# Seven products for eight: Strassen's scheme in three of eight K pairs of five 1024-column blocks

## The chip, the cores and the metric

The kernel runs on one core of one Trainium2 chip. The metric is the device time of one execution in microseconds (us). Engines are named as in the profile: PE is TensorE (PEld its weight loads), DVE VectorE, ACT ScalarE, SP the engine whose queue issues most DMAs.

## The reference

One decoder sub-layer on x of 256 tokens by 2048 channels, in float32:

```python
h = rms_norm(x, g_pre) * (1.0 + scale) + shift
proj = einsum('bsd,de->bse', h, w_in)            # 20032 columns
q_mla, kv_a, z_mla, qkv_dil, z_dil, gl_mla, gl_dil = split(proj, IN_SPLITS)
a  = mla_branch(q_mla, kv_a, ...) * silu(z_mla)
y_mla = einsum('bse,ed->bsd', a, w_mla_proj)
bb = dilated_branch(qkv_dil, ...) * silu(z_dil)
y_dil = einsum('bse,ed->bsd', bb, w_dil_proj)
merged = sigmoid(gl_mla) * y_mla + sigmoid(gl_dil) * y_dil
out = einsum('bsd,de->bse', merged, w_o)
x = x + gate * rms_norm(out, g_post)
```

The change touches three of the matrix products, each with K = 2048: the gate logits `gl_mla` (h by 2048 columns of w_in), the latent output `y_mla` (a by w_mla_proj), and the first 1024 of the 2048 columns of `out` (merged by w_o).

## The kernel before, in words

Every product of 256 tokens by a weight matrix is computed at float32 accuracy from float32r parts. Both operands are split into a high part (rounded to float32r) and a low part (the rest), and three matmul phases are summed: high by high, low activation by high weight, high activation by low weight. The token side (`hT`, `aT`, `mT`: the transposed activations, 16 K tiles of 128 rows by 256 tokens, in tiles `...h` and `...l`) is split once. The weight side is streamed: `load_split` (L243 to L253) loads two K tiles by 512 columns (512 KB) into a `raw` buffer (8 of them), ACT casts it to `whi` (L251), DVE subtracts to get `wlo` (L252); there are 4 buffers each of `whi` and `wlo`. `multiply` (L255) then issues 12 matmuls of 128x512: 3 phases, 2 K tiles, 2 token halves.

```python
for ph in range(3):
    wt = wlo if ph == 2 else whi
    part = opd.lo if ph == 1 else opd.hi
    for k in range(nk):
        for t in ts:
            T.matmul(acc[:, t, :n], opd.get(part, k0 + k, t), wt[:, k * n:(k + 1) * n], ...
```

`group` (L283) does this for 8 such chunks into one accumulator of two PSUM banks (`acc`, two accumulators in all), so one 512-column group is 96 matmuls. Four further banks (`b`) serve transposes and attention.

The end of the program runs, in this order: four pairs of groups `gd` and `yd`, which give `part`; four groups `gm` of gate logits (L797 to L801; ACT takes the sigmoid out of PSUM); four groups `ym` (L803 to L813), where DVE multiplies the accumulator with the sigmoid (L805), adds it to `part` (L806), PE transposes the sum (`pt_m`, L448) and it is split into `mTh` and `mTl` (L438, L439); `gate_finish` (L350 to L362) makes the output gate `gg` from two DMAs `bg`, issued on ACT's queue, and two PE products `pt_g`. Then four groups `o0` to `o3` of the output projection (L838 to L843) and a last one, followed by the norm and the store.

A scheduler in the tile framework puts each engine's instructions in order and adds the semaphore waits; each engine executes its own list in that order.

Of the kernel before, what the change touches and what calls it, by code (L numbers as in the profile page):

```python
# [73 lines left out]
def hybrid_block(ctx: ExitStack, tc: tile.TileContext, x, c, positions, w_ada, b_ada, g_pre, g_post,  # L74
                 w_in, g_kv, w_kv_b, w_mla_proj, w_dil_proj, w_o, table, out):
    nc = tc.nc
    V, A, T = nc.vector, nc.scalar, nc.tensor
# [719 lines left out]
    for n in range(4):  # L797
        acc = group(hT, win, KC, C_GLM + n * 512, 512, f"gm{n}")
        sg = slot([P, 2, 512], f"sgm{n}")
        A.activation(sg, acc, AF.Sigmoid)  # L800
        sgm.append(sg)  # L801
    mT_h, mT_l = [], []
    for n in range(4):  # L803
# [3 lines left out]
        hi = slot([P, 4, S], f"mTh{n}", F32R)  # L807
        lo = slot([P, 4, S], f"mTl{n}", F32R)
        transpose_split(part[n], hi, lo, f"m{n}")
        mT_h.append(hi)  # L810
        mT_l.append(lo)
        if n < 2:
            gate_finish(n)  # L813
# [72 lines left out]
```

## Time and profile before

| what | value |
|---|---|
| time, median of 3 runs | 1281.7 us (1280.17 to 1281.78) |
| the profiled execution: its own time | 1281.44 us |
| its span (first to last instruction) | 1279.7 us |
| PE busy | 1260.7 us, 99% of the span, 6101 instructions |
| PEld busy | 1050.0 us, 82% |
| DVE busy | 814.8 us, 64%, 1201 instructions |
| ACT busy | 601.9 us, 47%, 778 instructions |
| chain that ended last | PE 98%, DVE 1% |
| granted TensorE clock, mean | 0.995 |
| HBM | 214 GB/s over the span |

The span is what the profiler saw between the first and the last instruction; the execution's own time is 1.7 us longer. Busy time is the time in which an engine executed at least one instruction; instructions of DVE and ACT overlap their neighbours a little, so the sum of the single durations is larger than the busy time. The chain that ended last is followed back from the last instruction: at each step to the instruction whose end released it, or to the one before it on its engine.

### The profile page before, as it was taken

The page shows a single profiled execution, that of the slowest core. Times are in us where ns is not written, and L with a number is a line of the kernel's source. Part 1 is how long each engine was busy: PE and PEld are TensorE (multiplying, and loading weights), DVE is VectorE, ACT ScalarE, POOL GpSimd, SP SyncE. Part 2 cuts the span into 40 slices and gives each one's busy share as a digit, 9 for nine tenths or more (in the row PEclk, how much of TensorE's full clock was granted, in tenths as well). Part 3 has the DMA queues.
Part 4 walks back from the last instruction along what each step waited for, and adds up shares of the span by engine and source line. Part 5 has one row for each costly group of instructions (what it writes and reads, how often), then busy time and mean ns, then how long its engine had stood idle before and what let it go on. Part 6 is the DMA issues. An engine that isn't in the chain of part 4 may idle for free.

```text
span 1279.7 us, 16445 instructions
## 1 busy us (share of the span) xinstructions
PE 1260.7 (99%) x6101; PEld 1050.0 (82%) x6101; DVE 814.8 (64%) x1201; ACT 601.9 (47%) x778; POOL 0.2 (0%) x4
## 2 busy tenths in 40 slices
PE   7999999999999999999999999999999999999997
PEld 3788888888888888888888888888888888888886
DVE  4878887897984645556566576664544444565545
ACT  3556334433374544464554555555544444434442
POOL 0000000000000000000000000000000000000000
PEclk9999999999999999999999999999999999999999
DMA  9999988987554566656577585775566666666741
GB/s 329 313 304 334 317 277 281 309 269 233 171 160 119 156 190 195 185 158 215 164 223 243 171 281 175 225 229 161 154 196 196 192 191 196 206 214 187 256 155 67
DMA packets 158172, 275.01 MB, mean 215 GB/s; under 512 B 9542, under 2 KB 46860, under 8 KB 158092
## 3 DMA queue, kind: packets, MB, share of 16 engines
q1 hardware_dynamic: 156276, 268.43, 67.9%
q10 hardware_dynamic: 1816, 5.53, 1.2%
q8 instruction: 48, 0.79, 0.2%
q14 instruction: 32, 0.26, 0.1%
HBM read 271.83 MB, written 2.10 MB: 214 GB/s over the span
## 4 chain that ended last, share of the span: by engine, by line
PE 98%; DVE 1%; DMA 0%; ACT 0%; issue 0%; DVEq 0%; SPq 0%; ACTq 0%
PE acc_d L262 31%; PE acc_mq L262 10%; PE acc_zm L262 7%; PE acc_gd L262 7%; PE acc_ym L262 7%; PE acc_gm L262 7%; PE acc_o L262 6%; PE acc_kv L262 3%; PE acc_yd L262 3%; PE acc_zd L262 3%; PE acc_kva L262 2%; PE pv_D L543 1%; PE s_D L525 1%; PE s_M L722 1%; PE row L186 1%; PE pt_pD L487 1%
## 5 line engine op out<-in xcount | busy, mean ns | idle before, releaser
L251 ACT CAST whi_d<-raw_d 128x1024 fp32r<-128x1024 f32 (+1 forms) x156 | 152.7, 986 | 182.5 <-PE acc_d L262 138.7
L252 DVE TENSOR_TENSOR wlo_d<-raw_d,whi_d 128x1024 fp32r<-128x1024 f32 (+1 forms) x156 | 176.4, 1139 | 72.6 <-ACT whi_d L251 70.9
L262 PE MATMUL acc_d<-whi_d,hTh 128*128 128x512 f32 x576 | 160.2, 396 | 1.4 <-DVE d L636 1.4
L262 PE MATMUL acc_d<-whi_d,hTl 128*128 128x512 f32 x576 | 157.2, 391 | 0.0
L262 PE MATMUL acc_d<-wlo_d,hTh 128*128 128x512 f32 x576 | 156.2, 390 | 0.0
L262 PEld LDWEIGHTS acc_d<-whi_d,hTl 128*128 128x128 f32 x576 | 108.5, 189 | 23.8 <-DVE hTl L229 0.8
L262 PEld LDWEIGHTS acc_d<-wlo_d,hTh 128*128 128x128 f32 x576 | 108.4, 188 | 22.9
L262 PEld LDWEIGHTS acc_d<-whi_d,hTh 128*128 128x128 f32 x576 | 106.3, 188 | 22.7 <-issue 1.8
L252 DVE TENSOR_TENSOR wlo_mq<-raw_mq,whi_mq 128x1024 fp32r<-128x1024 f32 x48 | 58.7, 1223 | 49.4 <-ACT whi_mq L251 44.6
L193 DVE SCALAR_TENSOR_TENSOR ada<-raw_a,ccol,ada 128x512 f32<-128x512 f32 (+1 forms) x96 | 77.4, 807 | 17.1 <-DMA raw_a<-in_w_ada 16.0
L251 ACT CAST whi_mq<-raw_mq 128x1024 fp32r<-128x1024 f32 x48 | 50.4, 1050 | 59.6 <-PE acc_mq L262 26.9
L252 DVE TENSOR_TENSOR wlo_gm<-raw_gm,whi_gm 128x1024 fp32r<-128x1024 f32 x32 | 39.2, 1225 | 45.4 <-ACT whi_gm L251 45.4
L252 DVE TENSOR_TENSOR wlo_gd<-raw_gd,whi_gd 128x1024 fp32r<-128x1024 f32 x32 | 39.2, 1224 | 37.3 <-ACT whi_gd L251 37.3
L252 DVE TENSOR_TENSOR wlo_zm<-raw_zm,whi_zm 128x1024 fp32r<-128x1024 f32 x32 | 39.2, 1224 | 33.5 <-ACT whi_zm L251 27.5
L252 DVE TENSOR_TENSOR wlo_ym<-raw_ym,whi_ym 128x1024 fp32r<-128x1024 f32 x32 | 39.1, 1222 | 32.1 <-ACT whi_ym L251 32.1
L251 ACT CAST whi_ym<-raw_ym 128x1024 fp32r<-128x1024 f32 x32 | 33.7, 1055 | 51.0 <-PE acc_ym L262 41.0
L251 ACT CAST whi_gm<-raw_gm 128x1024 fp32r<-128x1024 f32 x32 | 33.8, 1055 | 49.6 <-PE acc_gm L262 43.9
L252 DVE TENSOR_TENSOR wlo_o<-raw_o,whi_o 128x1024 fp32r<-128x1024 f32 x28 | 34.2, 1224 | 35.4 <-ACT whi_o L251 32.4
L262 PE MATMUL acc_mq<-whi_mq,hTh 128*128 128x512 f32 x192 | 55.2, 409 | 0.0
L251 ACT CAST whi_gd<-raw_gd 128x1024 fp32r<-128x1024 f32 x32 | 33.6, 1051 | 40.9 <-PE acc_gd L262 18.7
L251 ACT CAST whi_zm<-raw_zm 128x1024 fp32r<-128x1024 f32 x32 | 33.6, 1051 | 39.5 <-PE acc_zm L262 12.5
L262 PE MATMUL acc_mq<-whi_mq,hTl 128*128 128x512 f32 x192 | 51.6, 391 | 0.0
(279 smaller groups left out, 2352.2 us busy)
## 6 DMA issues: line engine op xcount, KB each, us to landing
raw_d<-in_w_in SPq DMA_DIRECT2D x132, 512.0 KB, 4.5
raw_mq<-in_w_in SPq DMA_DIRECT2D x48, 512.0 KB, 4.5
raw_a<-in_w_ada SPq DMA_DIRECT2D x80, 256.0 KB, 4.7
raw_zm<-in_w_in SPq DMA_DIRECT2D x32, 512.0 KB, 4.2
raw_g<-in_w_ada SPq DMA_DIRECT2D x32, 512.0 KB, 4.4
raw_gd<-in_w_in SPq DMA_DIRECT2D x32, 512.0 KB, 4.4
raw_gm<-in_w_in SPq DMA_DIRECT2D x32, 512.0 KB, 4.4
raw_ym<-in_w_mla_proj SPq DMA_DIRECT2D x32, 512.0 KB, 3.9
```

Source lines behind the costliest of these rows:

```text
L186: T.matmul(row[0:1, j, 0:n], ccol[:, kk:kk + 1], v[:, k, j, :], start=kk == ROW_K[0], stop=kk == ROW_K[-1])
L193: V.scalar_tensor_tensor(flat, w, ccol[:, kk:kk + 1], flat, op0=ALU.mult, op1=ALU.add)
L251: A.copy(whi[:, :m], raw[:, :m])
L252: V.tensor_tensor(wlo[:, :m], raw[:, :m], whi[:, :m].bitcast(F32), ALU.subtract)
L262: T.matmul(acc[:, t, :n], opd.get(part, k0 + k, t), wt[:, k * n:(k + 1) * n], start=start and ph == 0 and k == 0, stop=stop and ph == 2 an ...
L487: T.transpose(pt[:, b, :], sm[:, (b0 + b) * P:(b0 + b + 1) * P], ident)
L525: T.matmul(sc[:, i * nk:(i + 1) * nk], qk[g][:, 0, t * P:(t + 1) * P], qk[g][:, 1, 0:nk], start=True, stop=True)
L543: T.matmul(pv, pT[:, b, :], dil[2, g, quad][:, kt, hs], start=b == 0, stop=b == nb - 1)
L722: T.matmul(sc[:, o:o + nk], qk[:, 0, t * P:(t + 1) * P], qk[:, 1, 0:nk], start=True, stop=False)
```

## The change

For five blocks of 1024 columns (two of `gm`, two of `ym`, the first half of the output projection) the two 512-column groups are computed together by `two_groups`. K goes in eight pairs of K tiles, and the string `PLAN = "SNSNSNNN"` says how each is done. An N pair is as before: two chunks (one for each 512 columns), 24 matmuls. An S pair is Strassen's scheme (Winograd's form) on the 2x2 blocks of the pair: K tile by token half on the one side, K tile by 512 columns on the other. It has seven products of three matmuls each, 21 in all. Its weight side needs four sums of raw weights (L359, L360, L363, L364, in place in the `raw` buffers) and four splits: `c` (512 columns), `d`, `e` and `f` (1024 each), which take one `whi` and one `wlo` buffer each. Four of the products gather in banks of their own (`p_...0` to `p_...3`, all four `b` banks), three in the accumulators. The token side needs sums too (`sums_of`): for each of the three S pairs a full-precision tile `af`, four sums `as`, and their split `ap`; they are made for h, a and merged once each, nine times in all. At the end of a block the banks are combined: one copy on ACT (L375), four additions of 512 columns and two of 1024 on DVE (L376 to L381). The sigmoid (L908), the product (L914) and the sum (L915) then follow as before, from SBUF. `gate_finish` is called once a block. The pool of small tiles `sp` is closed before `gm` and reopened as `sp2`.

```diff
+PLAN = "SNSNSNNN"
...
+    def products(bank, a, b, start, stop):
+
+        for i, (x, y) in enumerate(((a[0], b[0]), (a[1], b[0]), (a[0], b[1]))):
+            T.matmul(bank, x, y, start=start and i == 0, stop=stop and i == 2)
+
+    def sums_of(opd, i, name):
+
+
+        q, b = divmod(2 * i, 4)
+        full = slot([P, 2, S], f"af_{name}{i}")
+        V.tensor_add(full, opd.hi[q][:, b:b + 2, :].bitcast(F32), opd.lo[q][:, b:b + 2, :].bitcast(F32))
+        tmp = slot([P, 4, P], f"as_{name}{i}")
+        a11, a12, a21, a22 = [full[:, k, t * P:(t + 1) * P] for k in range(2) for t in range(2)]
+        V.tensor_add(tmp[:, 0, :], a12, a22)
+        V.tensor_sub(tmp[:, 1, :], tmp[:, 0, :], a11)
+        V.tensor_sub(tmp[:, 2, :], a11, a12)
+        V.tensor_sub(tmp[:, 3, :], a21, tmp[:, 1, :])
+        parts = sp.tile([P, 2, 4, P], F32R, tag="ap", bufs=5, name=f"ap_{name}{i}")
+        split(parts[:, 0], parts[:, 1], tmp)
+        return parts
...
+            first, final = i == first_s, i == last_s
+            (b11,) = both(r1, 512, "c")
+            products(banks[0], a(0, 0), b11, first, final)
+            V.tensor_sub(r1[:, l], r1[:, h], r1[:, l])
+            V.tensor_sub(r1[:, h], r2[:, h], r1[:, h])
+            b21, b22 = both(r2, 1024, "d")
+            t1, t3 = both(r1, 1024, "e")
+            V.tensor_sub(r2[:, h], r2[:, h], r1[:, l])
+            V.tensor_sub(r2[:, l], r2[:, l], r2[:, h])
+            products(banks[1], sm(0), t1, first, final)
+            products(banks[3], sm(2), t3, first, final)
+            t4, t2 = both(r2, 1024, "f")
+            products(banks[2], sm(1), t2, first, final)
+            products(acc[0][:, 1, :], a(1, 1), t4, begin((1, 0)), False)
+            products(acc[0][:, 0, :], a(1, 0), b21, begin((0, 0)), False)
+            products(acc[1][:, 0, :], sm(3), b22, begin((0, 1)), False)
+            tick()
+
+        u = [slot([P, 2, 512], f"u_{name}{j}") for j in range(2)]
+        A.copy(u[0][:, 0, :], banks[0])
+        V.tensor_add(u[1][:, 1, :], u[0][:, 0, :], banks[2])
+        V.tensor_add(u[0][:, 1, :], u[1][:, 1, :], banks[3])
+        V.tensor_add(u[1][:, 0, :], u[1][:, 1, :], banks[1])
+        V.tensor_add(u[1][:, 1, :], u[0][:, 1, :], banks[1])
+        for j in range(2):
+            V.tensor_add(u[j], u[j], acc[j])
+        return u
...
-    for n in range(4):
-        acc = group(aT, w_mla_proj[0], KC, n * 512, 512, f"ym{n}")
-        V.tensor_mul(sgm[n], sgm[n], acc)
-        V.tensor_add(part[n], part[n], sgm[n])
...
+    for m in range(2):
+        for j, y in enumerate(two_groups(aT, sums_a, w_mla_proj[0], KC, m * 1024, f"ym{m}")):
+            n = 2 * m + j
+            V.tensor_mul(sgm[n], sgm[n], y)
+            V.tensor_add(part[n], part[n], sgm[n])
...
+        gate_finish(m)
     mT = Opd(mT_h, mT_l)
...
+    sums = sums_for(mT, "m")
+    made = two_groups(mT, sums, w_o[0], KC, 0, "o")
     for i, (c0, n) in enumerate(blocks[:-1]):
-        acc = acc_tile(f"acc_o{i}")
-        run(acc, mT, w_o[0], 0, KC, c0, n, f"o{i}")
+        if i < 2:
+            acc = made[i]
+        else:
+            acc = acc_tile(f"acc_o{i}")
+            run(acc, mT, w_o[0], 0, KC, c0, n, f"o{i}")
```

What this does to the order is shown at the opening of the output projection. First DVE's list there before the change, from the last `wlo` of group `ym3` on (`o0_0`, `o0_2` ... are chunks of the output projection, `acc_ym3` the last accumulator of the stage before):

```order
L252 TENSOR_TENSOR wlo_ym3_14_9673<-raw_ym3_14_9670,whi_ym3_14_9672 128x1024
L252 TENSOR_TENSOR wlo_o0_0_9723<-raw_o0_0_9720,whi_o0_0_9722 128x1024
L252 TENSOR_TENSOR wlo_o0_2_9741<-raw_o0_2_9738,whi_o0_2_9740 128x1024
L252 TENSOR_TENSOR wlo_o0_4_9759<-raw_o0_4_9756,whi_o0_4_9758 128x1024
L805 TENSOR_TENSOR sgm3_9028<-sgm3_9028,acc_ym3_9543 128x1024
L252 TENSOR_TENSOR wlo_o0_6_9777<-raw_o0_6_9774,whi_o0_6_9776 128x1024
L806 TENSOR_TENSOR sgd3_8366<-sgd3_8366,sgm3_9028 128x1024
L252 TENSOR_TENSOR wlo_o0_8_9795<-raw_o0_8_9792,whi_o0_8_9794 128x1024
L439 TENSOR_TENSOR mTl3_9691<-pt_m30_9692,mTh3_9690 128x512
L439 TENSOR_TENSOR mTl3_9691<-pt_m31_9699,mTh3_9690 128x512
L252 TENSOR_TENSOR wlo_o0_10_9813<-raw_o0_10_9810,whi_o0_10_9812 128x1024
```

And DVE's list at the same place in the changed kernel, from the sum of the first half of the second `ym` block (`u_ym10`) on; `e` and `f` are splits of the first S pair of the output projection:

```order
L381 TENSOR_TENSOR u_ym10_9869<-u_ym10_9869,acc_ym10_9548 128x1024
L347 TENSOR_TENSOR wlo_oe0_9993<-raw_oa0_9975,whi_oe0_9992 128x1024
L914 TENSOR_TENSOR u_gm20_9159<-u_gm20_9159,u_ym10_9869 128x1024
L381 TENSOR_TENSOR u_ym11_9870<-u_ym11_9870,acc_ym11_9549 128x1024
L915 TENSOR_TENSOR sgd2_8145<-sgd2_8145,u_gm20_9159 128x1024
L914 TENSOR_TENSOR u_gm21_9160<-u_gm21_9160,u_ym11_9870 128x1024
L347 TENSOR_TENSOR wlo_of0_10005<-raw_ob0_9977,whi_of0_10004 128x1024
L543 TENSOR_TENSOR mTl2_9881<-pt_m20_9882,mTh2_9880 128x512
L543 TENSOR_TENSOR mTl2_9881<-pt_m21_9889,mTh2_9880 128x512
L915 TENSOR_TENSOR sgd3_8366<-sgd3_8366,u_gm21_9160 128x1024
L543 TENSOR_TENSOR mTl3_9899<-pt_m30_9900,mTh3_9898 128x512
L543 TENSOR_TENSOR mTl3_9899<-pt_m31_9907,mTh3_9898 128x512
```

Before, whole chunks of the output projection were split between the steps of the combination; now two splits of its first S pair (`e`, `f`) stand among ten steps of the combination. Three rows on (one chunk's split and the gate's additions), DVE's list reaches the token-side sums:

```order
L466 TENSOR_TENSOR gg1_9914<-gg1_9914,bg11_9923 128x1024
L295 TENSOR_TENSOR af_m0_9939<-mTh0_9502,mTl0_9503 128x512
L298 TENSOR_TENSOR as_m0_9941<-af_m0_9939 128x128
L300 TENSOR_TENSOR as_m0_9941<-af_m0_9939 128x128
L299 TENSOR_TENSOR as_m0_9941<-as_m0_9941,af_m0_9939 128x128
L295 TENSOR_TENSOR af_m2_9949<-mTh1_9520,mTl1_9521 128x512
L301 TENSOR_TENSOR as_m0_9941<-af_m0_9939,as_m0_9941 128x128
L298 TENSOR_TENSOR as_m2_9951<-af_m2_9949 128x128
L300 TENSOR_TENSOR as_m2_9951<-af_m2_9949 128x128
L299 TENSOR_TENSOR as_m2_9951<-as_m2_9951,af_m2_9949 128x128
L295 TENSOR_TENSOR af_m4_9959<-mTh2_9880,mTl2_9881 128x512
L543 TENSOR_TENSOR ap_m0_9946<-as_m0_9941,ap_m0_9946 128x512
```

All rows but the first are new; `ap_m0`, the split of the sums for the first S pair, is the last of them. On PE the output projection began before the change with

```order
L262 MATMUL acc_o0_9719<-whi_o0_0_9722,mTh0_9177 128x512 x4
L262 MATMUL acc_o0_9719<-whi_o0_0_9722,mTl0_9178 128x512 x4
L262 MATMUL acc_o0_9719<-wlo_o0_0_9723,mTh0_9177 128x512 x4
L262 MATMUL acc_o0_9719<-whi_o0_2_9740,mTh0_9177 128x512 x4
L262 MATMUL acc_o0_9719<-whi_o0_2_9740,mTl0_9178 128x512
L448 MATMUL pt_m30_9692<-tid_72,sgd3_8366 128x128 x4
L448 MATMUL pt_m31_9699<-tid_72,sgd3_8366 128x128 x4
L262 MATMUL acc_o0_9719<-whi_o0_2_9740,mTl0_9178 128x512 x3
L262 MATMUL acc_o0_9719<-wlo_o0_2_9741,mTh0_9177 128x512 x4
```

and begins now, behind two products with `f` (part t4), four with `f` and `d` and the transposes of both halves, with

```order
L463 MATMUL pt_g11_9920<-gacc2_6288,ones_87 128x512
L288 MATMUL p_o0_9971<-whi_oc0_9979,mTh0_9502 128x512
L288 MATMUL p_o0_9971<-whi_oc0_9979,mTl0_9503 128x512
L288 MATMUL p_o0_9971<-wlo_oc0_9980,mTh0_9502 128x512
L336 MATMUL acc_o0_9969<-whi_o0_2_10022,mTh0_9502 128x512 x4
L336 MATMUL acc_o0_9969<-whi_o0_2_10022,mTl0_9503 128x512 x4
L336 MATMUL acc_o0_9969<-wlo_o0_2_10023,mTh0_9502 128x512 x4
L288 MATMUL p_o1_9972<-whi_oe0_9992,ap_m0_9946 128x512 x2
L288 MATMUL p_o1_9972<-wlo_oe0_9993,ap_m0_9946 128x512
L288 MATMUL p_o3_9974<-whi_oe0_9992,ap_m0_9946 128x512 x2
```

Before, 17 matmuls stood ahead of the transposes that wait for the last group's sum, and everything behind them needed only weight chunks; now the products into `p_o1` and all behind them need `ap_m0`.

## Rows read from the trace of the kernel before

**Rows 1.** The page: busy time of each engine; shares of the last chain.

```profile
PE 1260.7 (99%) x6101; PEld 1050.0 (82%) x6101; DVE 814.8 (64%) x1201; ACT 601.9 (47%) x778; POOL 0.2 (0%) x4
...
PE 98%; DVE 1%; DMA 0%; ACT 0%; issue 0%; DVEq 0%; SPq 0%; ACTq 0%
```

**Rows 2.** Chain of waits, 995 to 1190 us: start us, us, work.

```profile
1000.60 87.04 PE acc_gm L262 x384
1087.64 25.62 PE acc_ym L262 x113
...
1138.52 1.72 PE pt_g L359 x4
...
1162.02 0.89 PE pt_m L448 x8
```

**Rows 3.** Chain of waits, whole span: the last group, 256 columns wide.

```profile
1258.59 5.77 PE acc_last L262 x48
```

**Rows 4.** Stretches: us, busy PE, PEld, DVE, ACT, POOL (x), clock, DMA, GB/s.

```profile
1000.00:1087.00 87.00, 87.00 (x385) 72.08 (x384) 40.33 (x33) 36.48 (x36) 0.00 (x0) 1.00 0.66 194
1087.00:1182.00 95.00, 95.00 (x425) 77.39 (x424) 55.18 (x51) 38.72 (x40) 0.00 (x0) 1.00 0.65 202
1182.00:1235.00 53.00, 53.00 (x239) 43.91 (x239) 29.18 (x28) 23.32 (x29) 0.00 (x0) 1.00 0.70 231
```

**Rows 5.** Groups by line and shape: busy us, mean ns of one, idle before.

```profile
L252 DVE TENSOR_TENSOR wlo_gm<-raw_gm,whi_gm 128x1024 fp32r<-128x1024 f32 x32 | 39.2, 1225 | 45.4 <-ACT whi_gm L251 45.4
...
L251 ACT CAST whi_gm<-raw_gm 128x1024 fp32r<-128x1024 f32 x32 | 33.8, 1055 | 49.6 <-PE acc_gm L262 43.9 <-PE acc_yd L262 5.7
...
L252 DVE TENSOR_TENSOR wlo_d<-raw_d,whi_d 128x512 fp32r<-128x512 f32 x24 | 16.5, 687 | 4.0 <-ACT whi_d L251 2.5 <-DMA raw_a<-in_w_ada 1.4
L251 ACT CAST whi_d<-raw_d 128x512 fp32r<-128x512 f32 x24 | 14.9, 620 | 15.4 <-PE acc_d L262 13.1 <-PE acc_zd L262 1.7 <-ACT whi_d L251 0.6
...
L422 DVE TENSOR_TENSOR rt_d<-d,sinD 128x128 f32<-128x128 f32 x12 | 3.4, 284 | 0.0
```

**Rows 6.** Timeline, a steady chunk of `gm`: start us, us, engine, work.

```profile
1001.35 1.07 PE L262 MATMUL acc_gm<-whi_gm,hTl 128*128 128x512 f32 x4
...
1002.45 1.05 ACT L251 CAST whi_gm<-raw_gm 128x1024 fp32r<-128x1024 f32 x1 [1.67 <-PE acc_gm L262]
...
1003.54 1.23 DVE L252 TENSOR_TENSOR wlo_gm<-raw_gm,whi_gm 128x1024 fp32r<-128x1024 f32 x1 [0.54 <-ACT whi_gm L251]
```

**Rows 7.** Timeline at the opening of the output projection.

```profile
1180.90 1.22 DVE L805 TENSOR_TENSOR sgm<-sgm,acc_ym 128x1024 f32<-128x1024 f32 x1 [1.31 <-PE acc_ym L262]
...
1182.04 1.22 DVE L252 TENSOR_TENSOR wlo_o<-raw_o,whi_o 128x1024 fp32r<-128x1024 f32 x1
...
1183.17 1.22 DVE L806 TENSOR_TENSOR sgd<-sgd,sgm 128x1024 f32<-128x1024 f32 x1
...
1184.44 0.91 PEld L448 LDWEIGHTS pt_m<-tid,sgd 128*128 128x128 f32 x8 [0.15 <-DVE sgd L806]
```

**Rows 8.** Timelines of ACT and DVE: a `bg` transfer, issue and use.

```profile
1138.56 0.35 ACTq L354 DMA_DIRECT2D bg<-in_b_ada  x1
...
1144.30 1.29 DVE L360 TENSOR_TENSOR gg<-pt_g,bg 128x512 f32<-128x512 f32 x2 [1.01 <-DMA bg<-in_b_ada]
```

**Rows 9.** Timelines of PE: the first matmuls of `acc_d`, and the last of all.

```profile
34.04 1.94 PE L262 MATMUL acc_d<-whi_d,hTh 128*128 128x512 f32 x4
36.02 2.07 PE L262 MATMUL acc_d<-whi_d,hTl 128*128 128x512 f32 x4
...
1269.46 0.64 PE L262 MATMUL acc_last<-wlo_last,mTh 128*128 128x256 f32 x4
```

**Rows 10.** Short stretches, columns as in rows 4.

```profile
36.00:38.00 2.00, 1.98 (x5) 1.59 (x6) 1.43 (x4) 0.53 (x2) 0.00 (x0) 0.50 0.94 328
...
1272.00:1273.00 1.00, 0.00 (x0) 0.00 (x0) 0.86 (x5) 0.00 (x0) 0.00 (x0) 1.00 0.11 38
1273.00:1274.00 1.00, 0.00 (x0) 0.00 (x0) 0.96 (x2) 0.00 (x0) 0.00 (x0) 0.84 0.00 0
```

More of the change, by code (lines that the diff above doesn't have):

```diff
@@ new lines, in load_raw, with two_groups, begin, both @@
+    def load_raw(w, k, c0, name):
+        raw = wp.tile([P, RAW], F32, tag="raw", bufs=RAW_BUFS, name=f"raw_{name}")
+        nc.sync.dma_start(raw, w[k * P:(k + 1) * P, c0:c0 + RAW])
+        return raw
+    def two_groups(opd, sums, w, nk, c0, name):
+        acc = [acc_tile(f"acc_{name}{j}") for j in range(2)]
+        banks = [tp_tile([P, 512], f"p_{name}{i}") for i in range(4)]
+        fresh = set()
+        last_s = PLAN.rindex("S")
+        first_s = PLAN.index("S")
+        def begin(key):
+            new = key not in fresh
+            fresh.add(key)
+            return new
+        marked = [i for i, m in enumerate(PLAN) if m == "S"]
+        for i, m in enumerate(PLAN[:nk // 2]):
+            k = 2 * i
+            end = 2 * i + 2 == nk
+            if m == "N":
+                for j in range(2):
+                    whi, wlo = load_split(w, k, 2, c0 + j * 512, 512, f"{name}{j}_{k}")
+                    for ph in range(3):
+                        wt, part = (wlo if ph == 2 else whi), (opd.lo if ph == 1 else opd.hi)
+                        for kk in range(2):
+                            for t in range(2):
+                                T.matmul(acc[j][:, t, :], opd.get(part, k + kk, t), wt[:, kk * 512:(kk + 1) * 512],
+                                         start=begin((t, j)), stop=end and ph == 2 and kk == 1)
+                    tick()
+                continue
+            r1, r2 = load_raw(w, k, c0, f"{name}a{k}"), load_raw(w, k + 1, c0, f"{name}b{k}")
+            l, h = slice(0, 512), slice(512, 1024)
+            def both(raw, n, nm):
+                hi = wp.tile([P, RAW], F32R, tag="whi", bufs=W_BUFS, name=f"whi_{name}{nm}{k}")
+                lo = wp.tile([P, RAW], F32R, tag="wlo", bufs=W_BUFS, name=f"wlo_{name}{nm}{k}")
+                A.copy(hi[:, :n], raw[:, :n])
+                V.tensor_tensor(lo[:, :n], raw[:, :n], hi[:, :n].bitcast(F32), ALU.subtract)
+                return [(hi[:, o:o + 512], lo[:, o:o + 512]) for o in range(0, n, 512)]
+            def a(kk, t):
+                return opd.get(opd.hi, k + kk, t), opd.get(opd.lo, k + kk, t)
+            def sm(q):
+                return sums[i][:, 0, q, :], sums[i][:, 1, q, :]
+            first, final = i == first_s, i == last_s
[14 more added lines that the diff above has]
+            products(acc[1][:, 0, :], sm(3), b22, begin((0, 1)), False)
+            tick()
+        u = [slot([P, 2, 512], f"u_{name}{j}") for j in range(2)]
[4 more added lines that the diff above has]
+        V.tensor_add(u[1][:, 1, :], u[0][:, 1, :], banks[1])
+        for j in range(2):
+            V.tensor_add(u[j], u[j], acc[j])
+        return u
@@ L283, in group, with sums_for @@
+    def sums_for(opd, name):
+        return {i: sums_of(opd, i, name) for i, m in enumerate(PLAN) if m == "S"}
     def group(opd, w, nk, c0, n, name):
@@ L795, in hybrid_block @@
         tick()
+    small.__exit__(None, None, None)
+    sp = ctx.enter_context(tc.tile_pool(name="sp2", bufs=2))
     sgm = []
-    for n in range(4):
[L798 to L801, printed above, removed]
-    mT_h, mT_l = [], []
-    for n in range(4):
-        acc = group(aT, w_mla_proj[0], KC, n * 512, 512, f"ym{n}")
-        V.tensor_mul(sgm[n], sgm[n], acc)
-        V.tensor_add(part[n], part[n], sgm[n])
[L807 to L813, printed above, removed]
+    sums = sums_for(hT, "h")
+    for n in range(0, 4, 2):
+        if n:
+            sums_a = sums_for(aT, "a")
+        for sg in two_groups(hT, sums, win, KC, C_GLM + n * 512, f"gm{n}"):
+            A.activation(sg, sg, AF.Sigmoid)
+            sgm.append(sg)
+    mT_h, mT_l = [], []
+    for m in range(2):
[3 more added lines that the diff above has]
+            V.tensor_add(part[n], part[n], sgm[n])
+            hi = slot([P, 4, S], f"mTh{n}", F32R)
+            lo = slot([P, 4, S], f"mTl{n}", F32R)
+            transpose_split(part[n], hi, lo, f"m{n}")
+            mT_h.append(hi)
+            mT_l.append(lo)
+        gate_finish(m)
     mT = Opd(mT_h, mT_l)
```

3 lines of the change are left out of this document (2 added, 1 removed).

## The prediction

> **What bounds the kernel now.** First the page: PE is busy 99% of the span and makes 98% of the chain that ended last [rows 1], so the time is the sum of PE's work. Then the chain through the changed stages: `gm` is one piece of 384 matmuls, 87.04 us, and `ym` runs on with only its transposes between [rows 2]. A 128x512 matmul thus costs 87.04 / 384 = 0.227 us there. A 128x256 one costs 5.77 / 48 = 0.120 [rows 3]: the price goes with the columns, so each 512-column matmul that is left out gives back 0.227 us, if PE then has other work ready. Whether it has is DVE's affair. DVE is busy 40.3 + 55.2 + 29.2 = 124.7 of 235 us in these stages [rows 4]; it waits for casts, the casts for PE to free a buffer [rows 5, 6]. So DVE has slack, and runs three chunks ahead of PE.
>
> **What is removed.** An S pair has 21 matmuls where an N pair has 24. Five blocks of three S pairs: 45 x 0.227 = 10.2 us off PE. The transposes (0.89 us for eight) and the gate's products (1.72 us) stay [rows 2].
>
> **What is added on DVE.** Prices [rows 5]: 1.22 us for 1024 columns, 0.69 for 512, 0.28 for 128; back to back the next starts 0.08 earlier, 1.14 after the one before [rows 7]. An S pair has splits of 512 and three of 1024 (4.35) and four sums of 512 (2.75) in place of two splits (2.45): 4.65 more, by 15 pairs 70 us. Token-side sums: nine times 0.69 + 4 x 0.28 + 0.69, 22.5 us. Combining: five times 4 x 0.69 + 2 x 1.22, 26 us. Together 174 instructions and 118 us, or 104 with the overlap of 0.08 each. DVE's load in the stages becomes 229 to 243 us, where PE's becomes 235 - 10.2 = 225. **DVE is then as full as PE.** Even without a single idle moment on DVE the stages take 229 us, and the gain is 6 us, not 10. ACT gets some 34 us more on 99 and stays far from full [rows 4, 5]. DMAs are as many and as large as before, the queue's order is the old one, and eight `raw` buffers cover them: nothing. Closing and reopening the small pool: nothing, since it falls where the attention is long over.
>
> **The openings.** Inside a block the two engines nearly balance: an S and an N pair take PE 45 x 0.227 = 10.2 us and DVE 6 splits and 4 sums, each sum waiting for the one before: 0.61 + 5 x 1.14 + 4 x 0.73 = 9.2 us. I take no cost for the steady S pairs. The balance fails where a block opens with an S pair, since there DVE has to combine the block before as well, and its list is executed in order. I walk the lists, with each instruction starting when the one before lets it (pitch above) and its input is there; a follower on another engine starts 0.04 us after the end [rows 6], and a matmul's result is there 0.16 us after its slot (four take 1.07, not 0.91 [rows 6]). T is counted from the end of the last block's last matmul.
>
> *Output projection.* The first accumulator is complete 12 matmuls before the end, so DVE begins L381 at -2.7, `e` at -1.6, L914 at -0.4, and so the second L381 only at 0.7, L915 at 1.9 (done 3.1), L914 at 3.0, `f` at 4.1 (done 5.4), two `mTl` to 6.5, L915 of the other half to 7.7. PE: waits 0.2 for the cast of `f`; two products; idle to 3.1 for `sgd2` (2.4); transposes 0.9; idle to 5.4 for `f` (1.4); four products; idle to 7.7 for `sgd3` (1.4); transposes, 1.7 us of gate products, three products with `c`, until 11.0; idle 1.0 for a cast whose buffer those have just freed; one chunk of 12, until 14.7. Now it needs `ap_m0`. DVE's list has the gate's additions ahead of it: `bg11` is issued on ACT behind the cast at 11.9, and such a transfer lands 1144.30 - 1138.56 = 5.7 us after issue [rows 8]: 17.6. Then L466 (1.2), `af` 0.7, the rest of the sums 1.5 and a cast of 0.6: 21.6. PE is idle 6.9 us, and 1.0 more for the low part. Sum: 0.2 + 2.4 + 1.4 + 1.4 + 1.0 + 6.9 + 1.0 = **14.3 us**. Before the change the same place had whole chunks split ahead, and PE stood 0.15 us [rows 7].
>
> *Second `ym` block.* The same combination, but no sums behind it: 0.2, 1.3 (the second L381 frees the accumulator at 1.9), 0.5, 1.4, 1.1 and 0.5 in the order of its waits: **5.0 us**.
>
> *The two `gm` blocks.* Before the first, DVE can begin on `c` at -8.4 (the buffer's high phases end at -9.1, the cast takes 0.6). The list up to the last raw sum has 12.3 us in it, the token-side sums of h and the product for `yd` among it: 3.9, and `f` is cast at 5.0. PE arrives after nine products, at 2.0: 3.0 idle. Before the second the list begins at -9.5 and holds 13.1 us, with the sums of a: 2.7 idle for `f`, 0.3 for `e`. Together **6.0 us**. *First `ym` block:* no sums, and `f` is cast at 0.8: nothing.
>
> Behind the last two openings DVE comes late to the second S pair too, as it still owes sums and additions: 2.4 us each by the walk, between nothing and the pair's own 4.8: **4.8**. Each of some 20 waits costs PE a restart (0.05 us to the weight load and 0.12 to the matmul after `sgd` was done [rows 7]); I take 0.1 each: **2**.
>
> **The clock.** The granted clock of 1.00 fell in the stretch that begins 3 us after PE's last matmuls [rows 9, 10]. The 6.9 us of waiting for `ap_m0` are longer, so I expect one fall to 0.50 (1.2 GHz) there. Its price: in the first 40 us eight matmuls of 512 took from 34.04 to 37.90 at 0.50 [rows 9, 10], 3.86 where 1.81 is usual: **2 us**.
>
> Sum: 14.3 + 5.0 + 6.0 + 4.8 + 2 + 2 = 34.1 lost, 10.2 gained: **+24 us**. The profiled execution took 1281.4 us (span 1279.7 and 1.7 around it), 0.3 under the median of 1281.7, so the forecast is **1305 us**, slower.
>
> **Rivals.** (1) *The openings are covered, and it is faster.* DVE enters each opening with a lead of some 8 us, and PE's list there has been put in the order of what is ready; the first `ym` block costs nothing even in my walk. It decides when all openings together cost under 10.2 us, a third of my sum. Then DVE's load is the bound, and the time is 1281.4 - 6 = 1275 us. Against it: the output's opening alone has 14 us, from a chain in which nothing runs beside. I give it 0.12. (2) *The openings cost just what is gained* (only the output's, at two thirds of its price): 1281 us, 0.04. (3) *The steady S pairs starve as well.* The second chunk of an N pair needs the buffers of `d`, whose products come last in an S pair; if DVE waits for them with the next S pair queued behind, it loses up to 2.8 us a turn, and the ten S pairs that I count at nothing come some 2 us late each: 1305 + 20 = 1325 us. The 1 us that DVE has to spare in 10.2 speaks for it, the scheduler's freedom to give out the first free buffer against it: 0.12. (4) *The clock falls at each opening*, not once: four more times 2 us, 1313 us. The waits of 3 us each are about as long as the clock lasted at the end [rows 9, 10], and between them PE works: 0.08. The Trainium skill, "TensorE: Matmul & The Clock Gate", section "HAM oscillation — how this bites in real kernels", says that a PE which waits between bursts of matmuls is throttled again and begins each burst at half clock; by that rule each of these openings would begin cold, and the time would be the 1313 us. The trace shows such a fall only behind the last matmul and in the sparse start. (5) *The change does not do what it says*: the changed list has 45 matmuls fewer, so no.
>
> **Numbers.** A change within 0.2% (2.6 us) is about what a measurement of this kernel can't tell from none. The forecast has 0.64, with 1295 to 1314 us as its own range (openings a third cheaper or dearer); with (3) and (4) that makes 0.84 slower, 0.04 within 0.2%, 0.12 faster. The range reaches from 1284 us (openings at two fifths) to 1326 us (rival 3 in full) and leaves out rival (1) and the tails beyond.
>
> **What would show it.** Right: some 3.0 us idle on PE before the product into `p_gm02` by ACT's cast of `f`, 5 us in pieces at `acc_ym10` and `pt_m00`, and one idle of 6 to 7 us before `p_o1` that ends with the cast of `ap_m0`; DVE over 90% busy from `gm` on; the chain's PE share down by 2 to 3 points with DVE in its place. Wrong: PE back to back through the openings (rival 1), or waits of 1 to 3 us in the second and third S pair of every block (rival 3), or a clock of 0.50 at each block (rival 4). It would be wrong altogether if DVE's in-place sums took less than the 0.69 us of other 512-column instructions.

## The result, and the profile after

The changed kernel takes **1302.97 us** (median of 4 runs, 1301.4 to 1306.8) where the kernel before took 1281.74 beside it: a ratio of 1.0169, 95% interval 1.0153 to 1.0185. It is slower by 21 us; forecast were 1305 us, between 1284 and 1326. The profiled execution took 1301.44 us, its span 1299.3.

The page of the changed kernel, the lines that answer to [rows 1]:

```profile
PE 1259.1 (97%) x6056; PEld 1041.6 (80%) x6056; DVE 919.3 (71%) x1375; ACT 632.6 (49%) x822; POOL 0.2 (0%) x4
...
PE 90%; DVE 6%; DMA 1%; ACT 1%; issue 1%; DVEq 0%; SPq 0%; ACTq 0%
```

45 matmuls fewer, 174 DVE instructions and 104.5 us of DVE more, as worked out. PE is busy for only 1.6 us less, though 10.2 us of matmuls are gone: matmuls that begin behind a wait or at a lower clock last longer, and eat the rest. Its share of the last chain falls by 8 points, and DVE's grows by 5.

The stretches of [rows 4], same columns, in the changed kernel:

```profile
1000.00:1087.00 87.00, 81.78 (x359) 66.51 (x358) 80.35 (x105) 47.89 (x52) 0.00 (x0) 1.00 0.60 194
1087.00:1182.00 95.00, 89.70 (x391) 71.08 (x390) 84.03 (x93) 47.71 (x52) 0.00 (x0) 1.00 0.57 188
1182.00:1235.00 53.00, 42.97 (x166) 31.50 (x165) 45.94 (x62) 23.08 (x27) 0.00 (x0) 0.90 0.57 192
```

DVE (fourth number) goes from 40, 55 and 29 us to 80, 84 and 46. PE stands still 5 us in each of the first two and 10 in the third, where the clock is 0.90.

What PE waited for between 995 and 1260 us in the changed kernel (waiting tile and line, released by; us in total, times, longest):

```profile
PE p_o L288 <- ACT ap_m L542: 3.9, 1, 3.9
PE p_gm L288 <- ACT whi_gm0f L346: 2.8, 1, 2.8
PE pt_m L552 <- DVE sgd L915: 2.6, 3, 2.2
PE p_gm L288 <- ACT whi_gm2f L346: 2.4, 1, 2.4
PE p_ym L288 <- ACT whi_ym1f L346: 1.6, 1, 1.6
PE acc_ym L288 <- DVE wlo_ym1f L347: 1.2, 1, 1.2
PE acc_o L288 <- DVE wlo_of L347: 1.2, 1, 1.2
PE acc_ym L288 <- DVE u_ym L381: 1.0, 1, 1.0
```

They are the waits that were forecast, at the forecast places: `whi_gm0f`, `whi_gm2f`, `u_ym`, `sgd`, `wlo_*f`, `ap_m`. The 1.6 us for `whi_ym1f` and 0.6 us for `whi_of` stand at the second S pair of the last two blocks, where the walk had 2.4 us each; all others stand at the openings, and behind the second S pair there are none. The chain of waits shows that, and where the stages begin and end (start us, us, work):

```profile
988.91 2.73 PE acc_yd L264 x12
...
1088.95 2.49 PE p_ym L288 x11
...
1099.15 2.72 PE p_ym L288 x12
1101.87 2.04 PE acc_ym L288 x9
1103.91 5.44 PE acc_ym L336 x24
...
1114.11 9.99 PE acc_ym L336 x44
...
1166.84 9.99 PE acc_ym L336 x44
...
1244.91 33.27 PE acc_o L264 x192
1278.18 5.78 PE acc_last L264 x48
```

A steady S pair is 12 and 9 matmuls in 2.72 + 2.04 = 4.76 us, 0.227 each, and an N pair 5.44: no time is lost there. The last group costs what it did [rows 3].

**One measure for all kernels.** PE's work up to the end of `yd` is the same everywhere, but the profiled executions reach its end anywhere between 999.4 and 1003.7 us. So stages are compared, not spans: from the end of `yd`'s 48 matmuls to the start of `acc_last`. Before, that is 1258.59 - 1000.60 = 258.0 us [rows 2, 3]. After, `yd` ends at 988.91 + 48 x 0.227 = 999.8, and the stage is 278.4. Without any loss it would have been 258.0 - 10.2 = 247.8: **30.6 us are lost**. By block, the 72 last matmuls of a block being 16.3 us, and each undisturbed block 41.5 (three S, five N pairs), with 3.5 more from transposes and gate products in the last two:

| block | from, to (us) | length | undisturbed | lost | forecast |
|---|---|---|---|---|---|
| two `gm` | 999.8, 1088.95 | 89.2 | 83.0 | 6.2 | 6.0 |
| first `ym` | 1088.95, 1130.4 | 41.5 | 41.5 | 0 | 0 |
| second `ym` | 1130.4, 1183.2 | 52.8 | 45.0 | 7.8 | 5.0 + 2.4 |
| output projection | 1183.2, 1244.91 | 61.7 | 45.0 | 16.7 | 14.3 + 2.4 + 2 (clock) |

In the last, the chain of the changed kernel runs over the gate's transfers, as the walk had it, though they land sooner:

```profile
1192.95 3.06 DMA bg<-in_b_ada
...
1196.06 3.83 DMA bg<-in_g_post
...
1199.97 1.22 DVE gg L466
```

The same place in PE's timeline (idle before, and who ended it, at the end of a row), and three stretches of 5 us there:

```profile
1186.34 1.09 PE L552 MATMUL pt_m<-tid,sgd 128*128 128x128 f32 x8 [2.16 <-DVE sgd L915]
1188.61 0.80 PE L288 MATMUL acc_o<-wlo_of,mTh 128*128 128x512 f32 x1 [1.18 <-DVE wlo_of L347]
1189.20 0.63 PE L288 MATMUL acc_o<-whi_od,mTh 128*128 128x512 f32 x1
1189.63 0.63 PE L288 MATMUL acc_o<-whi_od,mTl 128*128 128x512 f32 x1
...
1204.04 0.49 PE L288 MATMUL p_o<-whi_oe,ap_m 128*128 128x512 f32 x1 [3.87 <-ACT ap_m L542]
```

```profile
1185.00:1190.00 5.00, 2.49 (x11) 2.02 (x12) 5.00 (x7) 1.07 (x2) 0.00 (x0) 0.77 0.23 92
1190.00:1195.00 5.00, 4.75 (x15) 2.78 (x13) 2.27 (x3) 1.17 (x2) 0.00 (x0) 0.55 0.45 157
...
1205.00:1210.00 5.00, 4.80 (x15) 3.87 (x16) 4.90 (x12) 2.84 (x4) 0.00 (x0) 0.68 0.55 183
```

The clock fell twice: behind the waits of 2.2 and 1.2 us, where matmuls then start 0.43 apart instead of 0.227 (1.2 in place of 2.4 GHz), and again behind the wait of 3.9. Busy time times what the clock lacked gives an estimate of its price: 2.49 x 0.23 + 4.75 x 0.45 + 4.80 x 0.32 = 4.2 us.

### The profile page after: what moved, and what is told of

It is laid out like the page before. It is cut to its first block, busy times and chain, and to the rows that moved or that the text cites. A ratio compares the mean times of both kernels' runs of the same rounds, so it can differ in the third digit from the quotient of the medians.

```text
span 1299.3 us, 16628 instructions
## 1 busy us (share of the span) xinstructions
PE 1259.1 (97%) x6056; PEld 1041.6 (80%) x6056; DVE 919.3 (71%) x1375; ACT 632.6 (49%) x822; POOL 0.2 (0%) x4
## 4 chain that ended last, share of the span: by engine, by line
PE 90%; DVE 6%; DMA 1%; ACT 1%; issue 1%; DVEq 0%; SPq 0%; ACTq 0%
PE acc_d L264 30%; PE acc_mq L264 10%; PE acc_zm L264 7%; PE acc_gd L264 7%; PE acc_kv L264 3%; PE acc_zd L264 3%; PE acc_gm L336 3%; PE acc_ym L336 3%; PE acc_yd L264 3%; PE acc_o L264 3%; PE acc_kva L264 2%; PE acc_o L336 2%; PE pv_D L647 1%; PE s_D L629 1%; PE p_gm L288 1%; PE acc_gm L288 1%
## 5 line engine op out<-in xcount | busy, mean ns | idle before, releaser
L264 PE MATMUL acc_mq<-wlo_mq,hTh 128*128 128x512 f32 x192 | 51.5, 390 | 0.0
L740 DVE TENSOR_TENSOR d<-d,acc_d 128x1024 f32<-128x1024 f32 x34 | 41.3, 1216 | 10.4 <-PE acc_d L264 10.2
L452 DVE SCALAR_TENSOR_TENSOR gacc<-raw_g,ccol,gacc 128x512 f32<-128x512 f32 x60 | 44.9, 748 | 4.5 <-DMA raw_g<-in_w_ada 3.5
L264 PEld LDWEIGHTS acc_mq<-whi_mq,hTl 128*128 128x128 f32 x192 | 36.1, 188 | 8.1
L264 PEld LDWEIGHTS acc_mq<-wlo_mq,hTh 128*128 128x128 f32 x192 | 36.1, 188 | 7.8
```

The source lines that it names most:

```text
L452: V.scalar_tensor_tensor(acc, v[:, k, :], ccol[:, kk:kk + 1], acc, op0=ALU.mult, op1=ALU.add)
L740: V.tensor_add(d, d, acc[:, :, lo:hi])
```

## The experiments

The theory from the prediction: a block that opens with an S pair catches VectorE with its list unfinished, so the openings lose the time, not the S pairs as such. Its rivals: an S pair costs too much VectorE wherever it stands; a single transfer or the sums at the last opening are the cause; the clock is. The table has all runs, then each is told. "Lost" is the stage against 258.0 less 0.227 for each matmul left out.

| run | S pairs | matmuls less | median us | ratio to before [95%] | stage | lost |
|---|---|---|---|---|---|---|
| the change | 5 blocks, S first | 45 | 1302.97 | 1.0169 [1.0153, 1.0185] | 278.4 | 30.6 |
| `e1_n_first` | 5 blocks, N first | 45 | 1291.51 | 1.0085 [1.0071, 1.0099] | 269.1 | 21.3 |
| `e2_plain_o` | 4 blocks, S first | 36 | 1287.55 | 1.0047 [1.0033, 1.0060] | 263.8 | 14.0 |
| `e3_gate_early` | as the change | 45 | 1296.44 | 1.0128 [1.0106, 1.0150] | 276.6 | 28.8 |
| `e4_no_sums` | as the change | 45 | 1295.59 | 1.0114 [1.0098, 1.0130] | 271.7 | 23.9 |
| `e5_gm_n_first` | 2 blocks, N first | 18 | **1278.10** | 0.9975 [0.9965, 0.9985] | 254.3 | 0.4 |
| `e6_n_first_plain_o` | 4 blocks, N first | 36 | 1279.54 | 0.9982 [0.9973, 0.9992] | 256.3 | 6.4 |
| `e7_n_first_gate_early` | 5 blocks, N first | 45 | 1289.16 | 1.0067 [1.0050, 1.0084] | 265.5 | 17.7 |
| `e8_nn_first_gate_early` | 5 blocks, NN first | 45 | 1285.21 | 1.0027 [1.0016, 1.0039] | 261.0 | 13.2 |
| `e9_gm_four` | 2 blocks, four each | 24 | 1282.76 | 1.0008 [0.9999, 1.0017] | 259.4 | 6.9 |
| `e10_gm_ym0` | 3 blocks, N first | 27 | 1278.72 | 0.9974 [0.9965, 0.9982] | 254.0 | 2.1 |
| `e11_fill` | as the change | 45 | 1303.66 | 1.0178 [1.0152, 1.0205] | 279.0 | 31.2 |
| `e12_pool_merge` | as `e8` | 45 | 1295.17 | 1.0103 [1.0089, 1.0116] | 270.8 | 23.0 |

### A plain pair first

```diff
-PLAN = "SNSNSNNN"
+PLAN = "NSNSNSNN"
```

> Each block now opens with a plain K pair and takes its three sevens at the second, fourth and sixth pair (NSNSNSNN instead of SNSNSNNN). The number of matmuls, of VectorE instructions and of S pairs is that of the changed kernel. If the loss lies in the openings, where TensorE meets the 5 us of VectorE and ScalarE work of an S pair before any of it could be done ahead, most of the 20 us of waits of the five blocks go, and the clock falls at the output projection with them: 1273 to 1284 us. If an S pair costs too much VectorE wherever it stands, nothing changes but the place: 1298 to 1306 us.

Measured 1291.51 us: 11.5 less for the same work in another place, but short of the 1273 to 1284. Of its waits the three longest, in the columns used above:

```profile
PE p_o L288 <- ACT ap_m L542: 5.5, 1, 5.5
PE acc_o L288 <- ACT whi_of L346: 3.0, 1, 3.0
PE acc_ym L288 <- ACT whi_ym1f L346: 2.0, 1, 2.0
```

The `gm` openings fall to 0.9 us. What stays lies in the last two blocks, and there the chain of this kernel reads:

```profile
1187.34 6.72 DMA bg<-in_g_post
...
1198.22 4.52 PE p_o L288 x9
```

VectorE stands still for the last 4.5 of these 6.7 us, until the transfer has landed, and the nine products behind the wait take 4.52 us, 0.50 each where 0.227 is usual: the clock again. The first theory explains about a third of the loss (30.6 us become 21.3), the second is refuted as it stands, and the last block has a cause of its own.

### The output projection without sevens, and what holds its opening up

```diff
-    sums = sums_for(mT, "m")
-    made = two_groups(mT, sums, w_o[0], KC, 0, "o")
...
-        if i < 2:
-            acc = made[i]
```

> The first 1024 columns of the output projection go back to two plain groups, the four other blocks stay as changed. If the opening of the output projection is the dearest (some 10 us of waits and two falls of the clock there, against 2 us of matmuls saved), 1286 to 1293 us. If the loss is spread evenly over the five blocks, a fifth of 21 us goes: 1298 to 1300 us.

Measured 1287.55 us, 15.4 less than the change. With the 2.0 us of nine matmuls that it gives up, this block alone had lost 17.4 us, which the 16.7 of the table by blocks confirm. In its trace PE waits for nothing from 1180 us to the end of the block.

Two parts of that opening, one by one: the gate's transfers issued ahead of each `ym` block (their issue in a function of its own, called before `two_groups`; the sums over them stay where they were), and the sums of the merged operand left out.

```diff
     for m in range(2):
+        bgs = gate_load(m)
         for j, y in enumerate(two_groups(aT, sums_a, w_mla_proj[0], KC, m * 1024, f"ym{m}")):
...
-        gate_finish(m)
+        gate_finish(m, bgs)
```

> The two transfers of the gate's bias and weight rows are issued ahead of each ym block instead of after it, so that VectorE no longer stands still for a landing ahead of the sums that the output projection opens with. If the 3.9 us wait at the opening of the output projection was for those transfers, it goes, and the second fall of the clock with it: 1295 to 1300 us. If it was for VectorE's own work (merge, sums, low parts), the wait stays at 3 us or more: 1301 to 1305 us.

```diff
-    sums = sums_for(mT, "m")
+    sums = sums_a
```

> The three sums of the merged operand are left out and the output projection's S pairs take those of the attention operand, so this leaves out part of the computation: 18 VectorE and 3 ScalarE pieces, some 6.5 us of VectorE, at the opening of the output projection. If the sums and what stands ahead of them hold the opening up, the wait for the sums (3.9 us) goes and what stands behind them comes earlier: 1293 to 1299 us. If the operand's own pieces and low parts of the weights hold it up, 1300 to 1304 us.

Early transfers: 1296.44 us, 6.5 less, in the range of the first reading; but the wait stays 2.7 us long, close to the second, and the stage of its profiled execution is only 1.8 us shorter. That execution took 1303.25 us, 6.8 above the median of its kernel, and its stretches at the `gm` openings (columns as before) show where:

```profile
1004.00:1030.00 26.00, 23.19 (x90) 18.57 (x89) 22.52 (x29) 12.36 (x14) 0.00 (x0) 0.87 0.51 161
1030.00:1060.00 30.00, 27.57 (x115) 22.28 (x114) 27.61 (x41) 17.19 (x20) 0.00 (x0) 0.94 0.57 177
```

In this execution the clock fell behind the 2.8 us wait of the first `gm` block, where it stayed at 1.00 in the profiled execution of the change. It fell again behind the 2.4 us wait of the second. So the stage of `e3` is no measure of the transfer. Its waits are a better one: they add up to 16.3 us, in the change to 20.5. With the S pair first, the early transfers are worth 4.2 us of waits and, by the median, 6.5 us of time. Without the sums: 1295.59 us, 7.4 less, as expected; the wait for `ap_m` is gone, and that of 2.2 us for `sgd` with it. New are 1.1 us for `wlo_oe` and 1.0 for `u_ym`; the 1.2 for `wlo_of` and 0.9 for `whi_o` were there before, and `whi_of` grew from 0.6 to 1.3. Transfer and sums lie on one chain, so their prices don't add up.

### All blocks, with more ahead of the first S pair

`e1` with the early transfers, and the same with two plain pairs first (`PLAN = "NNSNSNSN"`).

> All five blocks with a plain pair first, and the gate's transfers issued ahead of the ym blocks. With the plain opening alone VectorE stood still 6.7 us for such a transfer, and TensorE 5.5 us for the sums behind it, then ran 30 us at a mean clock of 0.77. If the transfer is the cause, wait and clock fall go: 1279 to 1285 us. If VectorE's own work is what TensorE waits for, the gain is under 3 us: 1288 to 1292 us.

> As the one before, with two plain pairs at the opening and the sevens at the third, fifth and seventh pair (NNSNSNSN). If what is left there is VectorE's backlog at the openings, two plain pairs (10.9 us of TensorE, 4.9 us of VectorE) let it catch up: 2 to 5 us under that kernel. If the sum of VectorE's work in the latent blocks is the bound, or the late sevens delay the combination at the block's end, the same time or up to 3 us more.

Measured 1289.16 us, 2.4 under `e1`: with a plain pair first, the transfer is not what keeps the five blocks slow. The wait for `ap_m` shrank to 0.9 us, and the next one, for `whi_of`, grew from 3.0 to 5.3. Two plain pairs first: 1285.21, another 4 us less, as the first reading had it, and still above the kernel before. Its stretches ahead of the output projection:

```profile
1130.00:1175.00 45.00, 44.15 (x197) 35.17 (x197) 44.09 (x51) 23.87 (x27) 0.00 (x0) 1.00 0.61 197
1175.00:1190.00 15.00, 15.00 (x71) 11.62 (x69) 15.00 (x18) 3.94 (x7) 0.00 (x0) 1.00 0.66 222
```

DVE is busy 59.1 of 60 us. From the second latent block on, low parts, raw sums, combination, merge, gate and the sums of the merged operand fill it, and neither order of pairs tried brought all of it forward. I take that for the second cause, beside the openings. It is argued from this load, and from the runs below that leave S pairs out of these blocks and lose less; no run took the load away and kept the pairs without adding something else to the path.

### Sevens only where VectorE has room

Both with `PLAN = "NSNSNSNN"`: latent output and output projection plain (`e5`), the output projection plain (`e6`), and the second latent block plain as well (`e10`). `e9` is `e5` with `PLAN = "NSNSSNSN"`. `e5` and `e9` also make no sums of the attention operand, which nothing uses there.

> Sevens in the two gate-logit blocks alone, each opened by a plain K pair; latent output and output projection as in the kernel before. 18 matmuls less (4.1 us), and in these two blocks only 0.9 us of waits were left with the plain opening. If waits and the clock are all that eats the gain, 1277 to 1280 us, under the kernel before. If a block with sevens costs something else besides (its combination of products, which VectorE does ahead of the next block's low parts), 1281 to 1285 us.

> Sevens in the two gate-logit and the two latent-output blocks, each opened by a plain pair; the output projection plain. 36 matmuls less (8.2 us), against 0.9 us of waits in the gate blocks and 2.0 in the second latent block. If the openings are the loss, 1275 to 1279 us. If VectorE as a whole is full from the second latent block on (41.4 us busy of 45 there), its backlog moves into the plain output projection: 1281 to 1286 us.

> Sevens in the two gate blocks and the first latent block, each opened by a plain pair; second latent block and output projection plain. 27 matmuls less (6.1 us), against the 0.9 us of waits that the gate blocks show once the sums of the attention operand are made beside them. The combination of the first latent block falls on a plain opening. If openings and VectorE's backlog are all there is: 1275.5 to 1278 us, below the two versions with sevens in the gate blocks alone and in all four. If the combination and the merge delay the plain opening too: 1278.5 to 1281 us.

> Sevens in the two gate blocks alone, but in four of eight pairs (NSNSSNSN), two of them one right behind the other. 24 matmuls less (5.4 us instead of 4.1). With three, VectorE was busy 76.9 of 85 us there and TensorE never waited; a fourth adds some 4.6 us of VectorE to each block, so 86 of 85. If VectorE's room within a block is the limit, the two neighbours show waits of 1 us or more and the time is 1278 to 1282 us, no better than with three. If there is still room by the work done ahead, 1276 to 1277.5 us.

`e5` took 1278.10 us, within 1277 to 1280, and faster than the kernel before. Its stretch with the two `gm` blocks, and the chain right behind them:

```profile
1000.00:1085.00 85.00, 85.00 (x374) 69.79 (x373) 76.85 (x89) 48.48 (x52) 0.00 (x0) 1.00 0.63 203
```

```profile
1085.39 6.80 PE acc_ym L264 x30
```

PE doesn't wait at all; the two blocks take 1085.39 - 1001.99 = 83.4 us where the kernel before took 87.04 [rows 2]. 18 matmuls at 0.227 are 4.1 us, and 3.6 came: the price that the prediction put on a matmul holds where VectorE keeps up. `e10`, 27 matmuls less, came to 1278.72, above the 1275.5 to 1278 hoped for and within the other reading: 2.1 us are lost, about as much as the third block saves. But the time fits that other reading by chance: the first latent block takes its undisturbed 41.5 us (1087.40 to 1128.92), PE waits for nothing behind it, and 2.0 of the 2.1 us are lost in the two `gm` blocks (1002.38 to 1087.40, 85.0 us for 83.0), where `e10` makes the sums of the attention operand and `e5` does not. Its ratio and that of `e5` can't be told apart; no run made these sums at another place. `e6` at 1279.54 us lies above its 1275 to 1279: 6.4 us lost, some 2 of them in `gm`, the rest mainly at the second latent block, behind whose 2.0 us wait the clock fell (its timeline):

```profile
1139.54 0.50 PE L288 MATMUL acc_ym<-whi_ym1f,avh 128*128 128x512 f32 x1 [1.96 <-ACT whi_ym1f L346]
...
1142.27 0.63 PE L288 MATMUL p_ym<-wlo_ym1f,ap_a 128*128 128x512 f32 x1
1142.69 0.63 PE L288 MATMUL acc_ym<-wlo_ym1f,avh 128*128 128x512 f32 x1
```

These start 0.42 apart. `e9`, a fourth S pair: 1282.76 us, 0.8 above the 1278 to 1282 forecast for a full VectorE. Its stretch with the `gm` blocks, and its longest wait:

```profile
1000.00:1085.00 85.00, 82.02 (x348) 65.27 (x347) 81.29 (x99) 48.55 (x54) 0.00 (x0) 0.98 0.53 174
```

```profile
1010.59 0.82 PE L288 MATMUL p_gm<-whi_gm0f,ap_h 128*128 128x512 f32 x2 [1.88 <-ACT whi_gm0f L346]
```

DVE is at 81.3 of 85 us, PE waits 3 us, and six more matmuls saved cost 4.7 us. So a fourth S pair does cost when VectorE has no room left, and the second theory is right in that form. But the sign that was named, waits at the two neighbours, is the smaller part: they wait 0.8 us, while 1.9 stand at the first S pair of the first block, with a clock of 0.83 over 1010 to 1020 us behind them. There VectorE makes the sums of h for four pairs instead of three, and begins the raw sum of `f` (L363) 7.6 us after the end of `yd`, where `e5` begins it at 4.6.

### The clock, and the idle engine

`e11` is the changed kernel with matmuls that nobody reads, 8 ahead of the transposes of the third merged part and, here, 16 ahead of the products that wait for the sums:

```diff
             products(banks[0], a(0, 0), b11, first, final)
+            if name == "o" and first:
+                for j in range(16):
+                    T.matmul(banks[3], mT_h[0][:, 0, 0:P], mT_h[0][:, 0:2, :].rearrange("p a n -> p (a n)"),
+                             start=True, stop=True)
```

> The changed kernel with 24 matmuls added at the opening of the output projection whose results nobody reads (they are overwritten): 8 ahead of the transposes that waited 2.2 us for the merge, 16 ahead of the products that waited 3.9 us for the sums. They fill waits that are there anyway. If the falls of the clock after these waits cost time of their own (0.92 over 15 us and 0.87 over 30 us in the changed kernel, some 5 us), 1297 to 1300 us. If only the waits cost, the same as the changed kernel or up to 1 us more: 1301.5 to 1304 us.

Measured 1303.66 us, no gain. But the test says less than was meant, since the clock fell all the same (timeline, then a stretch):

```profile
1198.24 3.79 PE L361 MATMUL p_o<-mTh 128*128 128x512 f32 x16
...
1206.73 0.70 PE L288 MATMUL p_o<-whi_oe,ap_m 128*128 128x512 f32 x1 [1.98 <-ACT ap_m L546]
```

```profile
1205.00:1210.00 5.00, 2.81 (x6) 1.92 (x7) 5.00 (x15) 1.23 (x2) 0.00 (x0) 0.69 0.69 259
```

The waits of that opening shrink from 9.4 to 5.7 us in sum, and the stage is as long as before: the products with `ap_m0` begin 21.2 us after the end of the block before, in the change 20.9, whatever TensorE does meanwhile. No trace shows this opening with the clock up throughout, so the 4.2 us above stay an estimate. But one of the four executions of `e11` had a mean granted clock of 0.995 over its span (its profiled one 0.991, that of the kernel before 0.995) and still took 1301.26 us: the falls are worth a few of the 21 us, and are not what makes the change slow.

`e12` is `e8` with the merge (the two lines behind `two_groups`) on GpSimd.

> The version with two plain pairs first, sevens at the third, fifth and seventh, and the gate's transfers issued early, all five blocks; the merge (gate times latent output, and its sum with the other branch: 8 pieces of 1.13 us) goes from VectorE to GpSimd, which has nothing to do. If TensorE waits there because VectorE is full (44.1 of 45 and 15.0 of 15 us busy before the output projection), the 5 us of waits at that opening shrink to under 2 and the time to 1277 to 1282 us. If the merge itself, slower on GpSimd, becomes what the transposes wait for, 1285 to 1292 us.

Measured 1295.17 us, 10 more than `e8`. GpSimd's timeline, and its waiter:

```profile
1180.99 3.23 POOL L921 TENSOR_TENSOR u_gm<-u_gm,u_ym 128x1024 f32<-128x1024 f32 x1 [41.29 <-DVE u_ym L381]
...
1187.47 2.35 POOL L921 TENSOR_TENSOR u_gm<-u_gm,u_ym 128x1024 f32<-128x1024 f32 x1
```

```profile
PE pt_m L558 <- POOL sgd L922: 9.4, 4, 4.2
```

VectorE was relieved (36.3 of 45 us busy from 1130 on, where `e8` had 44.1), but a piece takes 2.35 to 3.23 us there and 1.14 to 1.22 on VectorE, and the merge lies on the path: PE now waits for it, 9.4 us. VectorE is slower beside it, too (its timeline):

```profile
1180.77 1.22 DVE L254 TENSOR_TENSOR wlo_o<-raw_o,whi_o 128x1024 fp32r<-128x1024 f32 x1
1181.90 1.21 DVE L381 TENSOR_TENSOR u_ym<-u_ym,acc_ym 128x1024 f32<-128x1024 f32 x1
1183.04 2.27 DVE L254 TENSOR_TENSOR wlo_o<-raw_o,whi_o 128x1024 fp32r<-128x1024 f32 x1
...
1190.85 1.97 DVE L347 TENSOR_TENSOR wlo_oc<-raw_oa,whi_oc 128x512 fp32r<-128x512 f32 x1
```

A low part of 1024 columns takes 2.27 us where 1.22 is usual, one of 512 takes 1.97 where 0.69 is. That is the second reading, and 3 us above its range of 1285 to 1292, so this run says nothing for or against VectorE's load as the cause in `e8`.

## Why the prediction was right, point by point

- **The gain per matmul.** 0.227 us for each one left out: right where PE doesn't wait (steady S pairs 4.76 us; `e5` 3.6 of 4.1).
- **VectorE's load.** 174 instructions and 104 us more were worked out with the overlap, 104.5 came. "As full as PE" was right in kind; busy were 89% of the 235 us, a little under the 90 given.
- **The openings.** `gm` 6.0, measured 6.2; first `ym` nothing, and nothing; second `ym` 5.0 + 2.4, measured 7.8; output projection 14.3 + 2.4, measured 16.7. The walk through the lists gave places and order. The sizes fit by block because the measured ones hold restarts and the clock as well, which the walk had not (see "The whole").
- **Mis-sized within the output projection.** The term of 6.9 us for `ap_m0` measured 3.9. `ap_m0` was ready 20.8 us after the end of the block before, not 21.6: the second transfer was issued 1.0 us later than in the walk, and landed 3.8 us after its issue, not 5.7 as [rows 8] had it. The larger part is PE's: it came to this wait at 17.0 us, not 14.7, made late by the clock and the restarts ahead of it. The 2.4 for the second S pair measured 0.6. In their place came two falls of the clock instead of one, 4.2 us instead of 2, and dearer restarts: each wait also delays the matmul that follows (the second one starts 0.34 us after the first at the waits of the second `ym` block, not 0.227, and 0.59 at the lower clock in the rows at 1188.61). So the sum of this block is partly right by errors that cancel.
- **The whole.** 34.1 us lost were forecast, 30.6 measured; 24 us slower forecast, 21 measured. The two parts of the sum missed in opposite directions. PE's waits add up to 20.5 us (5.2, 5.3 and 10.0 in the three stretches above) where the walk had 30.1; the other 10.1 us went into restarts and the lower clock, for which the prediction had 4. That the total came so near is in part luck. PE's share of the last chain fell by 8 points, not by the 2 to 3 named as a sign.
- **Rivals.** Covered openings (1) didn't come, and `e8` shows that even with two plain pairs first the five blocks end at 1285, not 1275: "then DVE's load is the bound" needs DVE's load by stage, and the last stage is overfull where the sum of all isn't. Starving steady pairs (3): no. A clock fall at each opening (4): not in the profiled execution of the change, whose `gm` and `ym` openings run at 1.00 behind waits of up to 2.8 us, nor in those of `e2`, `e4` and `e11` behind the same 2.8 us, but in that of `e3`. The prediction expected its one fall because 6.9 us are longer than the 3 us that the clock had lasted at the end [rows 9, 10]; it fell behind shorter waits too, of 2.2 and 1.2 us in the change and 2.0 in `e6`. The Trainium skill, "TensorE: Matmul & The Clock Gate", section "HAM oscillation — how this bites in real kernels", describes a kernel in which each burst behind a wait begins cold, with longer waits than most of these; the runs agree at the output projection, and at the `gm` opening in one profiled execution of the five with this wait.

## What to carry to other kernels

An algorithm that trades matmuls for elementwise work paid here only in the stages where the elementwise engine had room for it: count that engine's load stage by stage, epilogues included, not over the sum. Open each block with a pair that needs little of that engine, so that its list for the first costly pair is worked off under matmuls; here this alone was worth 11.5 us. Keep such blocks away from places where a merge, a transpose and the next block's operand follow one another: the two gate blocks alone, opened plainly, give 1278.1 us, the best shown, level with the version that adds the first latent block.
